# A list scheduler's table of durations replaced by the durations of the trace, in a two-layer diffusion step

## The chip, the cores and the metric

One core of a Trainium2 chip runs the whole program. The time is the device time of one execution in microseconds (us). Beside the timed runs there is one profiled execution, from which the rows of the trace are taken.

## The reference

The kernel computes one step of a small hybrid backbone with two layers on 384 tokens of width 1024: 256 latent tokens and 128 context tokens. Layer 0 projects once, then runs neighbourhood attention (8 heads) beside a bidirectional retention (8 heads). Layer 1 is a bidirectional gated linear recurrence (HGRN2, 8 heads of 128). Each is followed by a SwiGLU block, and every sub-layer is wrapped in two norms with modulation from a conditioning vector.

```python
hp = _rmsnorm(xp, norm_g[l, 0]) * (1.0 + sc1p) + sh1p
hs = _rmsnorm(xs, norm_g[l, 0]) * (1.0 + sc1s) + sh1s
...
xp = xp + gt1p * _rmsnorm(mp, norm_g[l, 1])
xs = xs + gt1s * _rmsnorm(ms, norm_g[l, 1])
hp = _rmsnorm(xp, norm_g[l, 2]) * (1.0 + sc2p) + sh2p
hs = _rmsnorm(xs, norm_g[l, 2]) * (1.0 + sc2s) + sh2s
xp = xp + gt2p * _rmsnorm(_swiglu(hp, w_ffn_in[l], w_ffn_out[l]), norm_g[l, 3])
xs = xs + gt2s * _rmsnorm(_swiglu(hs, w_ffn_in[l], w_ffn_out[l]), norm_g[l, 3])
```

## The kernel before

Activations stand transposed: 128 features on the partitions, 384 tokens along the free axis, eight such tiles k = 0 to 7. Weights come in 216 chunks of 128x1024 (eight 128x128 tiles each) by DMA into `wr`. Each chunk is split in two: ScalarE rounds it to `wh`, VectorE subtracts to get the rest `wl`. The input is split likewise into `hh` and `hl`. A product of float precision is then three matmuls, hh by wh, hh by wl and hl by wh. These are called **main products** here. There are 5088 of them, and the text counts them from 0: the first projection has 0 to 143, the two token-wise projections 144 to 287, the rest of layer 0's input projection up to 623, its output projection 624 to 815, the first SwiGLU 816 to 2399. Layer 1's input projection has 2400 to 3311, its output projection 3312 to 3503, and the second SwiGLU the rest.

Everything else on TensorE is side work: attention scores (`ka,qa`), transposes of the probabilities (`cb,as`), the retention (`qk`, `ro,vb`, `scr,cse`), the modulation (`mraw,sc` and, to turn the result, `ca,mev`), the sums of the norms (`scr,ca`, `acc,ca`, `rB,ca`), the spreading of a norm's factor over the partitions (`rs,cb`), and the eight mixers of layer 1. A mixer works through eight levels h = 0, 1, 2 up to 64. In each level TensorE multiplies the present pair of tiles (`XA` or `XB`, 64x64), VectorE picks from the product with a mask into `ac`, and ScalarE, GpSimd and VectorE make the next pair. After the last level come 128x128 products (`XB`, two transposes `cb,XB` and `cb,ZW`, `v,XA`, then nine into one bank beginning and ending with `at,v`) and a sum of squares (`scr,cb`). When four heads are through, `head_norm` takes a root, a reciprocal, splits the factors into `rh` and `rl`, and spreads them with `rh,bc` and `rl,bc`; then `o` is scaled, gated with `scr`, split into `hh` and `hl`, and only then can the output projection read it. The output projection begins with four of its eight outputs at once and walks over k, twelve main products to a k, so that its products 3312 to 3359 read heads 0 to 3, and those from 3360 on heads 4 to 7.

Nothing of this order is written by hand. Each piece of work is a generator (a stream) that yields operations. `Machine.run` (L174) looks at the next operation of each stream, computes when it could start from a clock for each engine and from the end of what it reads, and emits the one with the earliest start, in steps of 1/20 us, ties going by priority. `Machine.emit` (L127) then moves the engine's clock on by the operation's `cost`. So a cost decides nothing but the place of an instruction in the queue of its engine; on the chip each engine takes its queue in order and waits on semaphores. Added after an operation's end are fixed handover times (`LEAVE`, for VectorE 0.13 us), and 1.3 us for a change of ScalarE's function table.

A norm in mid program (class `Step`) has a path that nothing can hide: the last square is summed, a root and a reciprocal give the first factor, `rs,cb` spreads it, meanwhile three more sums feed a second root and reciprocal, a second `rs,cb` spreads that, and only then are `hh` and `hl` made for the next main product. While TensorE waits there, `keep_busy` sends fillers (`cb,ca`, results unused) and the modulation its products.

Of the kernel before, what the change touches and what calls it, by code (L numbers as in the profile page):

```python
# [30 lines left out]
F32R = mybir.dt.float32r  # L31
# [177 lines left out]
def width(ap):  # L209
    n = 1  # L210
    for s in ap.shape[1:]:
        n *= s
    return n


class Build:
# [4 lines left out]

    def mm(self, out, lhsT, rhs, start=True, stop=True):
        n = width(rhs)
        cost = n * (1 if rhs.dtype == F32R and n >= 256 else 4) / 2400
        cost *= {32: 0.3, 64: 0.56}.get(min(out.shape[0], lhsT.shape[0]), 1.0)
        return Op("PE", lambda: self.nc.tensor.matmul(out, lhsT=lhsT, rhs=rhs, start=start, stop=stop),  # L226
                  [out], [lhsT, rhs], cost + 0.004)

    def transpose(self, out, in_, ident):
        return Op("PE", lambda: self.nc.tensor.transpose(out, in_, ident), [out], [in_], 0.11)  # L230
# [1 line left out]
    def act(self, out, in_, func=AF.Copy, bias=None, scale=1.0, accum=None):  # L232
        kw = {"scale": scale}
        ins, outs = [in_], [out]
        if bias is not None:
            kw["bias"] = bias
            ins.append(bias)
        if not isinstance(scale, float):
            ins.append(scale)
        if accum is not None:  # L240
            kw["accum_out"] = accum
            outs.append(accum)
        table = None if func in (AF.Copy, AF.Identity, AF.Square) else func
        return Op("ACT", lambda: self.nc.scalar.activation(out, in_, func, **kw), outs, ins,  # L244
                  0.1 + width(in_) / 1200, table)

    def tt(self, out, a, b, op, pool=False):
        n = width(out)
        if pool:
            return Op("POOL", lambda: self.nc.gpsimd.tensor_tensor(out=out, in0=a, in1=b, op=op), [out], [a, b],  # L250
                      0.12 + n * 0.0021)
        return Op("DVE", lambda: self.nc.vector.tensor_tensor(out=out, in0=a, in1=b, op=op), [out], [a, b],  # L252
                  0.06 + n / 960)

    def ts(self, out, a, s1, op0, s2=None, op1=None):
        ins = [a] + [s for s in (s1, s2) if s is not None and not isinstance(s, float)]
        kw = {} if op1 is None else {"op1": op1}
        return Op("DVE", lambda: self.nc.vector.tensor_scalar(out=out, in0=a, scalar1=s1, scalar2=s2, op0=op0, **kw),  # L258
                  [out], ins, 0.19 + width(out) / 1920)

    def stt(self, out, a, s, b, op0, op1, accum=None):
        ins = [a, b] + ([] if isinstance(s, float) else [s])
        outs = [out] + ([] if accum is None else [accum])
        kw = {} if accum is None else {"accum_out": accum}
        return Op("DVE", lambda: self.nc.vector.scalar_tensor_tensor(out=out, in0=a, scalar=s, in1=b, op0=op0, op1=op1, **kw),  # L265
                  outs, ins, 0.1 + width(out) / 960)

    def copy(self, out, a):
        return Op("DVE", lambda: self.nc.vector.tensor_copy(out, a), [out], [a], 0.06 + width(out) / 960)

    def pcopy(self, out, a):
        return Op("POOL", lambda: self.nc.gpsimd.tensor_copy(out, a), [out], [a], 0.1 + width(out) * 0.0017)

    def recip(self, out, a):
        return Op("DVE", lambda: self.nc.vector.reciprocal(out, a), [out], [a], 0.1 + width(out) * 0.0065)

    def reduce_max(self, out, a):
        return Op("DVE", lambda: self.nc.vector.tensor_reduce(out=out, in_=a, axis=AX.X, op=ALU.max), [out], [a],
                  0.06 + width(a) / 960)

    def select(self, out, mask, data):
        return Op("DVE", lambda: self.nc.vector.copy_predicated(out, mask, data), [out], [mask, data, out],
                  0.06 + width(out) / 960)

    def zero(self, out):
        return Op("POOL", lambda: self.nc.gpsimd.memset(out, 0.0), [out], [], 0.1 + width(out) * 0.001)
# [91 lines left out]
def constants():  # L378
# [46 lines left out]
    for n, h in enumerate(LEVELS):  # L425
        m[:, n] = (s == tt) if h == 0 else ((s // (2 * h) == tt // (2 * h)) & (s // h != tt // h))
# [1298 lines left out]
```

## Time and profile before

| | us |
|---|---|
| timed runs | 1123.0, 1123.99, 1126.69 |
| median | 1123.99 |
| the profiled execution's own time | 1122.49 |
| its span, first to last instruction | 1120.3 |
| TensorE busy in the span | 1083.7 |
| VectorE busy | 811.7 |
| ScalarE busy | 551.7 |
| GpSimd busy | 131.8 |

Between span and time of the profiled execution lie 2.2 us that the trace doesn't show. In rows of the profile PE is TensorE, PEld its weight loads, DVE VectorE, ACT ScalarE, POOL GpSimd and SP the queue that issues DMAs. A row of the timeline has start, duration, engine, line, operation, what is written and read, the count of merged instructions, and in brackets idle time of the engine just before it with what ended it. Matmuls overlap in the pipeline, so that main products that each last 0.34 us follow each other at about half of that. A matmul in plain float appears as two passes.

### The profile page before, as it was taken

The page shows a single profiled execution, that of the slowest core. Times are in us where ns is not written, and L with a number is a line of the kernel's source. Part 1 is how long each engine was busy: PE and PEld are TensorE (multiplying, and loading weights), DVE is VectorE, ACT ScalarE, POOL GpSimd, SP SyncE. Part 2 cuts the span into 40 slices and gives each one's busy share as a digit, 9 for nine tenths or more (in the row PEclk, how much of TensorE's full clock was granted, in tenths as well). Part 3 has the DMA queues.
Part 4 walks back from the last instruction along what each step waited for, and adds up shares of the span by engine and source line. Part 5 has one row for each costly group of instructions (what it writes and reads, how often), then busy time and mean ns, then how long its engine had stood idle before and what let it go on. Part 6 is the DMA issues. An engine that isn't in the chain of part 4 may idle for free.

```text
span 1120.3 us, 18505 instructions
## 1 busy us (share of the span) xinstructions
PE 1083.7 (97%) x7172; PEld 1008.3 (90%) x7172; DVE 811.7 (72%) x1508; ACT 551.7 (49%) x1034; POOL 131.8 (12%) x143
## 2 busy tenths in 40 slices
PE   7999999999999999999999999999999999999996
PEld 5768877989999999999987988889989999999995
DVE  2599986688999998995887589996786444443434
ACT  4587654667333333323765456656575333333331
POOL 1220000000000000333024145341000000000001
PEclk9999999999999999999999999999999999999998
DMA  9966554254766666664432322212323333333331
GB/s 349 365 217 231 187 191 149 94 189 162 249 228 242 231 241 228 223 235 141 165 127 81 108 86 85 91 65 102 113 77 137 126 130 115 132 123 123 131 113 57
DMA packets 49687, 180.44 MB, mean 161 GB/s; under 512 B 6560, under 2 KB 13728, under 8 KB 43072
## 3 DMA queue, kind: packets, MB, share of 16 engines
q1 hardware_dynamic: 49536, 179.18, 45.5%
q8 instruction: 56, 0.92, 0.3%
q14 instruction: 31, 0.25, 0.1%
q0 software_dynamic: 64, 0.08, 0.0%
HBM read 174.79 MB, written 3.41 MB: 159 GB/s over the span
## 4 chain that ended last, share of the span: by engine, by line
PE 80%; DVE 12%; ACT 3%; issue 2%; DMA 2%; SPq 1%; POOL 0%; DVEq 0%; ACTq 0%; POOLq 0%
PE bank L226 79%; DVE wl L252 2%; DVE mscr L265 1%; DMA mraw<-in_w_mod 1%; ACT scr L244 1%; DVE XB L252 1%; PE bank L230 1%; DVE XA L252 1%; DVE scr L258 1%; DMA msb<-in_cB 1%; SPq L291 1%; DVE scr L252 0%; DVE T L258 0%; DVE XA L258 0%; DVE x L252 0%
## 5 line engine op out<-in xcount | busy, mean ns | idle before, releaser
L226 PE MATMUL bank<-hh,wh 128*128 128x384 f32 (+1 forms) x1248 | 429.2, 344 | 0.6 <-ACT hh L244 0.4
L226 PE MATMUL bank<-hh,wl 128*128 128x384 f32 (+1 forms) x1248 | 424.2, 340 | 0.0
L226 PE MATMUL bank<-hl,wh 128*128 128x384 f32 (+1 forms) x1248 | 391.8, 344 | 0.0
L252 DVE TENSOR_TENSOR wl<-wr,wh 128x1024 fp32r<-128x1024 f32 x216 | 273.2, 1266 | 127.8 <-ACT wh L244 127.6
L244 ACT ACTIVATE wh<-wr 128x1024 fp32r<-128x1024 f32 x216 | 228.1, 1057 | 150.9 <-PE bank L226 103.9
L226 PEld LDWEIGHTS bank<-hh,wh 128*128 128x128 f32 x1248 | 237.1, 190 | 7.8 <-ACT scr L244 2.4
L226 PEld LDWEIGHTS bank<-hl,wh 128*128 128x128 f32 x1248 | 232.0, 189 | 5.6 <-issue 1.7
L226 PEld LDWEIGHTS bank<-hh,wl 128*128 128x128 f32 x1248 | 236.7, 190 | 0.3
L265 DVE SCALAR_TENSOR_TENSOR mscr<-mraw,msb 128x1024 bf16<-128x1024 f32 x128 | 159.5, 1246 | 4.2 <-ACT msb L244 3.2
L226 PE MATMUL bank<-gh,wl 128*128 128x384 f32 x352 | 118.2, 336 | 1.9 <-DVE wl L252 1.9
L226 PE MATMUL bank<-gh,wh 128*128 128x384 f32 x352 | 117.6, 334 | 0.0
L226 PE MATMUL bank<-gl,wh 128*128 128x384 f32 x352 | 117.6, 334 | 0.0
L226 PEld LDWEIGHTS bank<-gh,wl 128*128 128x128 f32 x352 | 66.1, 188 | 3.5 <-DVE wl L252 3.5
L226 PEld LDWEIGHTS bank<-gh,wh 128*128 128x128 f32 x352 | 66.1, 188 | 0.0
L226 PEld LDWEIGHTS bank<-gl,wh 128*128 128x128 f32 x352 | 66.1, 188 | 0.0
L244 ACT ACTIVATE fs<-bank 128x384 f32<-128x384 f32 x44 | 21.1, 491 | 88.0 <-PE bank L226 88.0
L252 DVE TENSOR_TENSOR fs<-bank,fs 128x384 f32<-128x384 f32 x44 | 24.1, 557 | 38.0 <-PE bank L226 38.0
L244 ACT ACTIVATE gh<-fs 128x384 fp32r<-128x384 f32 x44 | 22.5, 520 | 58.0 <-DVE fs L252 58.0
L244 ACT ACTIVATE scr<-bank 128x384 f32<-128x384 f32 x44 | 21.9, 498 | 54.7 <-PE bank L226 54.7
L250 POOL TENSOR_TENSOR rB<-x,fy 128x384 f32<-128x384 f32 x1 | 1.8, 1782 | 381.4 <-DVE fy L258 381.4
L250 POOL TENSOR_TENSOR x<-x,fy 128x384 f32<-128x384 f32 x4 | 4.5, 1150 | 347.5 <-DVE fy L252 347.5
L250 POOL TENSOR_TENSOR ZW<-XB,TA 128x192 f32<-128x192 f32 x48 | 37.7, 806 | 37.8 <-ACT XA L244 17.8
(251 smaller groups left out, 1325.8 us busy)
## 6 DMA issues: line engine op xcount, KB each, us to landing
mraw<-in_w_mod SPq DMA_DIRECT2D x48, 1024.0 KB, 6.1
wr<-in_w_ffn_in SPq DMA_DIRECT2D x88, 512.0 KB, 3.3
wr<-in_w_ffn_out SPq DMA_DIRECT2D x44, 512.0 KB, 3.2
wr<-in_w_in_odd SPq DMA_DIRECT2D x40, 512.0 KB, 3.2
wr<-in_w_in_even SPq DMA_DIRECT2D x28, 512.0 KB, 4.4
wr<-in_w_out_even SPq DMA_DIRECT2D x8, 512.0 KB, 3.3
wr<-in_w_out_odd SPq DMA_DIRECT2D x8, 512.0 KB, 3.3
bias<-in_bias SPq DMA_DIRECT2D x8, 384.0 KB, 3.9
```

The source lines that it names most:

```text
L226: return Op("PE", lambda: self.nc.tensor.matmul(out, lhsT=lhsT, rhs=rhs, start=start, stop=stop), [out], [lhsT, rhs], cost + 0.004)
L230: return Op("PE", lambda: self.nc.tensor.transpose(out, in_, ident), [out], [in_], 0.11)
L244: return Op("ACT", lambda: self.nc.scalar.activation(out, in_, func, **kw), outs, ins, 0.1 + width(in_) / 1200, table)
L250: return Op("POOL", lambda: self.nc.gpsimd.tensor_tensor(out=out, in0=a, in1=b, op=op), [out], [a, b], 0.12 + n * 0.0021)
L252: return Op("DVE", lambda: self.nc.vector.tensor_tensor(out=out, in0=a, in1=b, op=op), [out], [a, b], 0.06 + n / 960)
L258: return Op("DVE", lambda: self.nc.vector.tensor_scalar(out=out, in0=a, scalar1=s1, scalar2=s2, op0=op0, **kw), [out], ins, 0.19 + width(o ...
L265: return Op("DVE", lambda: self.nc.vector.scalar_tensor_tensor(out=out, in0=a, scalar=s, in1=b, op0=op0, op1=op1, **kw), outs, ins, 0.1 + ...
L291: return Op("SP", lambda: self.nc.sync.dma_start(out, in_), [a for a in here if a is out], [a for a in here if a is in_], n / 355e3)
```

## The change

The functions that make operations give each its `cost`. The change replaces these figures for nearly all kinds and touches nothing else. A few of the lines:

```diff
-        cost = n * (1 if rhs.dtype == F32R and n >= 256 else 4) / 2400
+        cost = n / 2200 if rhs.dtype == F32R and n >= 256 else n / 600
...
-                  0.1 + width(in_) / 1200, table)
+                  0.17 + width(in_) / 1200, table)
...
-                  0.06 + n / 960)
+                  0.15 + n / 960)
```

A main product of 384 columns goes from 0.164 to 0.177 us, a VectorE operation of 384 columns from 0.46 to 0.55 (from 1.13 to 1.22 for a weight split), a ScalarE operation of 384 columns from 0.42 to 0.49, a GpSimd product of 192 columns from 0.52 to 0.76.

The main products keep their order. All else is placed anew around them. Counts on the engines stay, but for fillers (56 `cb,ca` before, 52 after, in fours) and ScalarE's table loads (18 before, 15 after). Three places follow.

TensorE at the last head of layer 1, before. The first factor `rh`, `rl` of heads 4 to 7 is spread here, in the middle of the main products of the last input projection (`hh,wh` and the like):

```order
L226 MATMUL bank_69<-hl,wh_110 128x384
L226 MATMUL bank_70<-rh,bc_4560 128x384
L226 MATMUL bank_70<-rl,bc_4560 128x384
L226 MATMUL bank_69<-hh,wh_110 128x384
L226 MATMUL bank_69<-hh,wl_113 128x384
L226 MATMUL bank_69<-hl,wh_110 128x384
L226 MATMUL bank_64<-hh,wh_111 128x384
L226 MATMUL bank_64<-hh,wl_114 128x384
L226 MATMUL bank_65<-hh,wh_111 128x384
L226 MATMUL bank_65<-hh,wl_114 128x384
L226 MATMUL bank_67<-rh,bc_4560 128x384
L226 MATMUL bank_67<-rl,bc_4560 128x384
```

The same after, from the last main product ahead of k = 4 of the output projection (3359) to the first behind it (some rows of the nine products, and of the four spreads, are not shown):

```order
L226 MATMUL bank_65<-hl,wh_112 128x384
L226 MATMUL bank_69<-XB_4584 64x64 x6
L226 MATMUL bank_68<-XA_4583 64x64 x6
L226 MATMUL bank_63<-XB_4584 128x128 x2
L230 MATMUL bank_63<-cb,XB_4584 128x128
L230 MATMUL bank_63<-cb,ZW_4585 128x128
L226 MATMUL bank_63<-v,XA_4583 128x128 x2
L226 MATMUL bank_64<-at_4587,v 128x128
...
L226 MATMUL bank_64<-scr_91,cb 32x96 x4
L226 MATMUL bank_69<-rh,bc_4562 128x384
L226 MATMUL bank_69<-rl,bc_4562 128x384
...
L226 MATMUL bank_67<-hh,wh_110 128x384
```

The four spreads stood at main products 3309, 3316, 3326 and 3335 and now all stand at 3360. So do the last two levels of head 7 (`XB`, `XA`) and its products; those of 128x128 began at 3258 before. No main product stands between them.

VectorE in layer 0, where the retention's norm feeds the output projection, before (`rs` is the norm's factor, `qk` the retention's output, `va` its gate, `wl` a weight split):

```order
L275 RECIPROCAL rs_88<-rs_88 128x96
L252 TENSOR_TENSOR hl<-qa,hh 128x384
L252 TENSOR_TENSOR scr_91<-rs_88,cb 128x384
L252 TENSOR_TENSOR wl_115<-wr_109,wh_112 128x1024
L252 TENSOR_TENSOR hl<-qa,hh 128x384
L252 TENSOR_TENSOR qk<-qk,bank_66 128x384
L252 TENSOR_TENSOR qk<-qk,va 128x384
```

And after (`mscr` is a modulation product by VectorE, of 1024 columns):

```order
L275 RECIPROCAL rs_88<-rs_88 128x96
L265 SCALAR_TENSOR_TENSOR mscr_132,macc_134<-mraw_105,msb_131 128x1024
L252 TENSOR_TENSOR wl_114<-wr_108,wh_111 128x1024
L252 TENSOR_TENSOR scr_92<-rs_88,cb 128x384
L265 SCALAR_TENSOR_TENSOR mscr_132,macc_134<-mraw_105,msb_131 128x1024
L252 TENSOR_TENSOR qk<-qk,bank_70 128x384
L265 SCALAR_TENSOR_TENSOR mscr_132,macc_134<-mraw_105,msb_131 128x1024
L252 TENSOR_TENSOR qk<-qk,va 128x384
```

Three modulation products have come into this path. On TensorE the spread that feeds `qk<-qk,bank` has gone from main product 635 to 672, and 672 is the first that reads its result.

TensorE at the norm ahead of the second SwiGLU (main product 3504), before:

```order
L226 MATMUL bank_65<-scr_95,ca 32x96 x4
L226 MATMUL bank_68<-rB,ca 32x96 x4
L226 MATMUL bank_64<-mraw_105,sc 32x256 x4
L226 MATMUL bank_68<-scr_93,ca 32x96 x4
L226 MATMUL bank_68<-acc_86,ca 32x96 x4
L226 MATMUL bank_68<-scr_92,ca 32x96 x4
L226 MATMUL bank_66<-rs_88,cb 128x96 x4
L226 MATMUL bank_64<-mraw_104,sc 32x256 x8
L226 MATMUL bank_67<-rs_89,cb 128x96 x4
```

And after:

```order
L226 MATMUL bank_70<-scr_92,ca 32x96 x4
L226 MATMUL bank_67<-mraw_105,sc 32x256 x4
L226 MATMUL bank_65<-rs_88,cb 128x96 x4
L226 MATMUL bank_66<-rB,ca 32x96 x4
L226 MATMUL bank_66<-scr_91,ca 32x96 x4
L226 MATMUL bank_66<-acc_86,ca 32x96 x4
L226 MATMUL bank_66<-scr_95,ca 32x96 x4
L226 MATMUL bank_67<-mraw_104,sc 32x256 x8
L226 MATMUL bank_67<-ca,mev 128x2 x4
L226 MATMUL bank_69<-rs_89,cb 128x96 x4
```

The four sums that feed the second factor have gone behind the spread of the first (`rs_88,cb`). At the norm of main product 816 the same has happened, with `ca,mev` also ahead of them; at 2400 these rows have kept their order.

More of the change, by code (lines that the diff above doesn't have):

```diff
@@ L223, in mm @@
         n = width(rhs)
-        cost = n * (1 if rhs.dtype == F32R and n >= 256 else 4) / 2400
+        cost = n / 2200 if rhs.dtype == F32R and n >= 256 else n / 600
         cost *= {32: 0.3, 64: 0.56}.get(min(out.shape[0], lhsT.shape[0]), 1.0)
         return Op("PE", lambda: self.nc.tensor.matmul(out, lhsT=lhsT, rhs=rhs, start=start, stop=stop),
-                  [out], [lhsT, rhs], cost + 0.004)
+                  [out], [lhsT, rhs], cost + 0.002)
     def transpose(self, out, in_, ident):
@@ L250, in tt @@
             return Op("POOL", lambda: self.nc.gpsimd.tensor_tensor(out=out, in0=a, in1=b, op=op), [out], [a, b],
-                      0.12 + n * 0.0021)
+                      0.3 + n * 0.0024)
         return Op("DVE", lambda: self.nc.vector.tensor_tensor(out=out, in0=a, in1=b, op=op), [out], [a, b],
-                  0.06 + n / 960)
+                  0.15 + n / 960)
     def ts(self, out, a, s1, op0, s2=None, op1=None):
@@ L258, in ts @@
         return Op("DVE", lambda: self.nc.vector.tensor_scalar(out=out, in0=a, scalar1=s1, scalar2=s2, op0=op0, **kw),
-                  [out], ins, 0.19 + width(out) / 1920)
+                  [out], ins, 0.21 + width(out) / 1920)
     def stt(self, out, a, s, b, op0, op1, accum=None):
@@ L265, in stt @@
         return Op("DVE", lambda: self.nc.vector.scalar_tensor_tensor(out=out, in0=a, scalar=s, in1=b, op0=op0, op1=op1, **kw),
-                  outs, ins, 0.1 + width(out) / 960)
+                  outs, ins, 0.15 + width(out) / 960 + (0.0 if accum is None else 0.08))
     def copy(self, out, a):
-        return Op("DVE", lambda: self.nc.vector.tensor_copy(out, a), [out], [a], 0.06 + width(out) / 960)
+        return Op("DVE", lambda: self.nc.vector.tensor_copy(out, a), [out], [a], 0.15 + width(out) / 960)
     def pcopy(self, out, a):
@@ L274, in recip @@
     def recip(self, out, a):
-        return Op("DVE", lambda: self.nc.vector.reciprocal(out, a), [out], [a], 0.1 + width(out) * 0.0065)
+        return Op("DVE", lambda: self.nc.vector.reciprocal(out, a), [out], [a], 0.13 + width(out) * 0.0065)
     def reduce_max(self, out, a):
         return Op("DVE", lambda: self.nc.vector.tensor_reduce(out=out, in_=a, axis=AX.X, op=ALU.max), [out], [a],
-                  0.06 + width(a) / 960)
+                  0.15 + width(a) / 960)
     def select(self, out, mask, data):
         return Op("DVE", lambda: self.nc.vector.copy_predicated(out, mask, data), [out], [mask, data, out],
-                  0.06 + width(out) / 960)
+                  0.15 + width(out) / 960)
     def zero(self, out):
```

## The prediction

> **What bounds the kernel now.** First the head of the page, which gives each engine's busy time in the span.
>
> ```profile
> span 1120.3 us, 18505 instructions
> PE 1083.7 (97%) x7172; PEld 1008.3 (90%) x7172; DVE 811.7 (72%) x1508; ACT 551.7 (49%) x1034; POOL 131.8 (12%) x143
> ```
>
> TensorE is busy for 1083.7 of 1120.3 us, and its operations stay the same but for four fillers. So the change can only move what TensorE loses: some 37 us without work, half-clock stretches, and the extra time of going from main products to side work and back. Where an engine beside it is full is told by the windows (from:to, length, busy of PE, PEld, DVE, ACT, POOL with instruction counts, granted clock, DMA share, GB/s).
>
> ```profile
> 480.00:500.00 20.00, 18.83 (x104) 17.87 (x105) 19.83 (x29) 6.40 (x9) 6.37 (x4) 1.00 0.67 239
> 700.00:720.00 20.00, 19.72 (x170) 18.22 (x171) 19.97 (x46) 12.96 (x30) 7.00 (x10) 1.00 0.22 72
> ```
>
> VectorE is full in the first SwiGLU (480 to 500) and in the mixers (700 to 720); only there can its order hold TensorE. What TensorE waits for is told by the waits (total us, times, longest).
>
> ```profile
> PE bank L226 <- DMA mraw<-in_w_mod: 9.3, 2, 6.9
> PE bank L226 <- DVE wl L252: 2.0, 6, 0.6
> PE bank L226 <- DVE XB L252: 1.6, 4, 0.7
> PE bank L230 <- ACT qk L244: 0.6, 1, 0.6
> ```
>
> The first is the start (6.9) and one wait of 2.4 in mid program. All four together are 13.5 us, 6.9 of them at the start where nothing can be done: little to gain. A scheduler that places side work so that nothing waits is near its floor; one that places it wrongly has no floor. So I count what becomes late.
>
> **Is the new table nearer the truth?** These two rows follow each other on VectorE.
>
> ```profile
> 753.77 1.21 DVE L252 TENSOR_TENSOR wl<-wr,wh 128x1024 fp32r<-128x1024 f32 x1
> 754.91 0.55 DVE L252 TENSOR_TENSOR scr<-bank,scr 128x384 f32<-128x384 f32 x1
> ```
>
> The split lasts 1.21, but the next starts 1.14 after its start: the old cost (1.13) is the engine's step, the new one (1.22) the duration. So the model's VectorE gets slower than the chip's by about 0.08 an operation, and side work is put later than it could be, by 30 to 50 main products in the attention and 10 to 140 in the mixers.
>
> **The start.**
>
> ```profile
> 11.31 1.94 PE L226 MATMUL bank<-mraw,sc 128*32 128x256 f32 x16
> 13.18 0.69 PE L226 MATMUL bank<-hh,wh 128*128 128x386 f32 x1
> 14.03 0.37 ACT L244 ACTIVATE mev<-bank 128x256 f32<-128x256 f32 x1
> ```
>
> The first main product begins at 13.18. In the new order the second `ca,mev` stands ahead of it, and reads the `mev` that ScalarE ends at 14.40. The main product then begins some 1.3 later (0 if ScalarE comes to it sooner, 1.6 at most with the product's own time): **+1.3**.
>
> **The wait for the modulation.**
>
> ```profile
> 162.92 0.44 PE L226 MATMUL bank<-hl,wh 128*128 128x384 f32 x1
> 165.72 1.02 PE L226 MATMUL bank<-mraw,sc 128*32 128x256 f32 x8 [2.36 <-DMA mraw<-in_w_mod]
> 166.00:168.00 2.00, 2.00 (x20) 0.70 (x12) 0.51 (x2) 0.00 (x0) 0.00 (x0) 0.50 0.95 375
> 168.00:170.00 2.00, 2.00 (x20) 0.95 (x12) 2.00 (x4) 0.00 (x0) 0.00 (x0) 0.69 0.35 47
> ```
>
> At main product 528 TensorE waits 2.36 us for a load that SP has issued behind weights. The product now stands at 672, 144 main products of 0.18 us or 26 us later; on SP its load goes back behind only some weights and `ro<-qk`. The wait goes: **-2.4**. After it the granted clock is 0.50 for 2 us and 0.69 for 2: (1-0.50)x2+(1-0.69)x2 = 1.6, **-1.6**. Next there are the main products of 528 themselves, whose weights ended no wait in this row. The attention's wait for `qk` goes too, as its transposes move back: **-0.6**.
>
> By the Trainium skill, "TensorE: Matmul & The Clock Gate", What's actually happening, the clock falls after an idle window of about 3.4 us. The wait here was 2.36 and the clock fell all the same, so the trace speaks against that length as a threshold. By the page only the wait is saved, and the sum would be 1.6 higher.
>
> **Switches.** Going into side work and back has a price.
>
> ```profile
> 765.61 0.34 PE L226 MATMUL bank<-hh,wl 128*128 128x384 f32 x1
> 765.79 0.34 PE L226 MATMUL bank<-hl,wh 128*128 128x384 f32 x1
> 766.06 0.57 PE L226 MATMUL bank<-XA 128*64 128x64 f32 x12
> 766.56 0.44 PE L226 MATMUL bank<-hh,wh 128*128 128x384 f32 x1
> ```
>
> Main products start 0.18 apart; the `XA` products start 0.27 after one, and the main product behind them lasts 0.44 where the others last 0.34: 0.09 + 0.10, about 0.2 for a switch. The new order has 70 runs of side work in the mixers where there were 83: 13 x 0.2, **-2.6**. In the attention 32 for 42, half of them transposes that I price at nothing: 10 x 0.1, **-1.0**. The waits for `XB` go, as their readers stand later: **-1.6**.
>
> **The first output projection.** The path from spread to `hh` now has a `mscr` in it.
>
> ```profile
> 79.16 1.22 DVE L265 SCALAR_TENSOR_TENSOR mscr<-mraw,msb 128x1024 bf16<-128x1024 f32 x1
> 201.67 0.56 DVE L252 TENSOR_TENSOR qk<-qk,bank 128x384 f32<-128x384 f32 x1 [0.92 <-PE bank L226]
> 202.86 0.56 DVE L252 TENSOR_TENSOR qk<-qk,va 128x384 f32<-128x384 f32 x1 [0.63 <-ACT va L244]
> 203.68 0.51 ACT L244 ACTIVATE hh<-qk 128x384 fp32r<-128x384 f32 x1
> ```
>
> The spread moves from main product 635 to 672, and 672 itself reads the result. TensorE, with all main products queued behind, waits 0.56 + 1.22 + 0.56 + 0.51 = 2.85: **+2.8** (0 if the spread's k = 4 wasn't the first needed, 4 with handovers and a second `mscr`).
>
> **The three norms.**
>
> ```profile
> 238.44 1.05 PE L226 MATMUL bank<-ca,mev 128*128 128x2 f32 x8
> 239.53 0.17 DVE L252 TENSOR_TENSOR mod<-bank,bmod 128x8 f32<-128x8 f32 x1 [1.11 <-PE bank L226]
> 820.65 0.35 PE L226 MATMUL bank<-rB,ca 128*32 128x96 f32 x8
> 822.81 1.13 PE L226 MATMUL bank<-rs,cb 128*128 128x96 f32 x8 [0.28 <-DVE rs L275]
> ```
>
> At 3504 the four sums for the second factor now wait behind `rs,cb` of the first: two groups of two sums by the row of 0.35 (0.17 each, 0.7), and about 1.0 of the 1.13 of `rs,cb` itself, whose end overlaps: **+1.7**. At 816 `ca,mev` (1.05) comes on top, but the 1.11 that VectorE waited for it is no longer in the path: **+1.8**. At 2400 the order is kept: 0. Below 0 these can't go, for the second factor needs all four sums; the fillers hide nothing, since they stand behind.
>
> **The first SwiGLU.** Its six waits for `wl` came where by the order a `mscr` of 1.22, priced at 1.17, stood ahead of a split: **-2.0** from the row above. But three more splits go ahead of the last `mscr` (from split 94 to 97 of 102), with VectorE at 19.83 of 20.
>
> **The last head.** This term decides. In the new order nothing of a main product stands between head 7's sixth level and the spreads, all at 3360, and 3360 reads what they give. TensorE takes its queue in order, so this chain can't begin before 3359 has been issued. Its pieces, from the rows of the same operations before:
>
> ```profile
> 764.98 0.36 DVE L282 COPY_PREDICATED ac<-msk,bank 128x192 f32<-128x192 uint8 x1
> 770.07 0.48 DVE L258 TENSOR_SCALAR XA<-XB,TA 128x128 f32<-128x128 f32 x2
> 770.90 0.61 PE L226 MATMUL bank<-XB 128*128 128x128 f32 x4
> 774.88 0.39 PE L226 MATMUL bank<-at,v 128*128 128x128 f32 x2
> 777.98 1.28 ACT L244 ACT_TABLE_LOAD   x1
> 778.21 0.37 PE L226 MATMUL bank<-scr,cb 128*32 128x96 f32 x8
> 779.28 0.38 ACT L244 ACTIVATE ss<-ss,eps 128x96 f32<-128x96 f32 x1
> 779.69 0.75 DVE L275 RECIPROCAL ss<-ss 128x96 f32<-128x96 f32 x1 [0.71 <-ACT ss L244]
> 782.43 0.55 DVE L252 TENSOR_TENSOR rl<-rr,rh 128x384 fp32r<-128x384 f32 x1
> 783.89 0.34 PE L226 MATMUL bank<-rh,bc 128*128 128x384 f32 x1
> 784.44 0.61 DVE L265 SCALAR_TENSOR_TENSOR o<-o,gnm,bank 128x384 f32<-128x384 f32 x1
> ```
>
> - The mask's select (764.98) to the last level's end (770.55) took 5.6 with other work in it; the operations alone give some 1.6. I take 3.3, with one `wl` ahead of them.
> - `XB` to `at,v`: 770.90 to 774.88 is 4.0, with 12 main products of 0.18 (2.2) in it. Where these hid part of ScalarE's copies they don't come off in full: between 1.8 and 4.0 I take 2.3.
> - `at,v` to `scr,cb`: 774.88 to 778.21 is 3.3, with 7 main products (1.3) in it: between 2.0 and 3.3 I take 2.6, the middle.
> - `scr,cb` to the reciprocal, past the table load: 1.5. Reciprocal's start to the end of `rl` (782.98): 3.3 with a gate ahead, 2.3 without.
> - `rh,bc` 0.4; then `o` (0.61), the gate (384 columns, 0.56 as `qk<-qk,va`) and `hh` (0.51, as at 203.68), with three handovers of 0.2: 2.3.
>
> That is 3.3 + 2.3 + 2.6 + 1.5 + 2.3 + 0.4 + 2.3 = 14.7. In it lies TensorE's own work, which was paid before as well: two levels 1.0, the 128x128 products 3.1, sums and spreads 1.6: 5.7. So **+9.0** (7 with the first three pieces at the low ends but for a `wl`, 13.6 with the rows' own spacing). After so long a wait the clock falls as it did at 166: **+1.6**.
>
> The row of 777.98 and that of 779.28 are back to back: the load ends at 779.26. The Trainium skill, "ScalarE: Activation LUTs", What ACT_TABLE_LOAD costs, puts a drain of 1.38 us beside the 1.28 of the load. No drain stands behind the load here; by the page the chain, and the sum, would be 1.4 longer.
>
> **The sum.** 1.3 - 2.4 - 1.6 - 0.6 - 1.0 + 2.8 + 1.8 + 1.7 - 2.0 - 1.6 - 2.6 + 9.0 + 1.6 = **+6.4**. On the profiled execution's 1122.5 (span 1120.3 and 2.2 around it) that is 1128.9; the median of the runs, 1124.0, lies 1.5 above that execution, so the forecast is **1130.4**. A measurement of this kernel tells about 0.3%, 3.4 us, from no change: the bounds are 1120.6 and 1127.4.
>
> **Rivals.**
>
> 1. *Switches are dear: faster.* I price 23 switches and the `XB` waits at 5.2 in all. A switch that also waits for `XB` costs 0.2 + 1.6/4 = 0.6. If every saved one were worth 0.50, the gains would cancel the sum; from 0.65 on the change is faster by over 0.3%. At 0.7 the sum is 6.4 - (16.1 - 5.2) = -4.5: **1119.5**. For it: VectorE is full at 700 to 720, so that side work there is often not ready. Against: TensorE is busy for 19.72 of the same 20 us. Chance 0.13.
> 2. *The late chains are shorter than the rows: no change.* ScalarE and VectorE have little to do around 3360, the chain costs 7 and the clock holds (-3.6), and the spread at 672 is covered by what stands between (-2.8): sum 0.0, **1124.0**. For it: the rows were taken with other work between. Against: no operation of the chain can be left out. Chance 0.20.
> 3. *VectorE overflows in the first SwiGLU: slower still.* The three splits pushed behind `mscr` meet an engine at 19.83 of 20; TensorE waits some 2 a split, +6, and the clock falls at 672 and 816 too, +3.2: **1139.6**. Against: the waits there were only 2.0. Chance 0.12.
>
> The change not doing what it says is part of all: the table holds durations where the engine's step is shorter, as shown above.
>
> **How the numbers follow.** The forecast has 0.55; its own range is 1126.5 to 1136, the tail from 7 to 13.6. It is inside 0.3% with 0.03. Faster: 0.13. Same: 0.20 + 0.03 = 0.23. Slower: 0.52 + 0.12 = 0.64. The range reaches to rivals 1 and 3: 1119 to 1141.
>
> **What would show it.** In the timeline after, a wait of 7 to 11 us in pieces between main products 3359 and 3360, near 795, with the clock at half behind it; no wait for `mraw` near 165; the first main product near 14.5; a wait for ScalarE's `hh` near 210; the stretches without main products ahead of 816 and 3504 each longer by nearly 2; fewer waits for `wl` and `XB`. If the wait at 3360 is under 4 us, or the mixers gain over 10, the prediction is wrong.

## The result and the profile after

| | before | after |
|---|---|---|
| median of the timed runs, us | 1125.21 | 1142.47 |
| range, 4 runs each | 1123.0 to 1126.69 | 1138.96 to 1144.14 |
| ratio | | 1.0151, 95% interval 1.0134 to 1.0167 |

The first three runs of before are those of the table above, and a fourth (1126.43) has been added. The change makes the kernel 17.3 us slower. The sign was forecast; the size was not: +6.4 stood in the sum, and 1142.5 lies above the range, which ended at 1141.

The head of the page of the changed kernel, and the mean granted clock over its span (0.993 before):

```profile
span 1142.4 us, 18492 instructions
PE 1091.7 (96%) x7164; PEld 1016.9 (89%) x7164; DVE 807.1 (71%) x1508; ACT 546.6 (48%) x1031; POOL 138.1 (12%) x143
core 0: 1142.4 us, clock 0.985
```

TensorE does less work (7164 instructions for 7172) and is busy 8 us longer: its operations got slower, not more. The other 14 us are idle. Its waits after (in us, times, longest), some of them:

```profile
PE bank L226 <- DVE rs L275: 7.5, 6, 2.0
PE bank L226 <- DMA mraw<-in_w_mod: 7.4, 2, 7.2
PE bank L226 <- DVE wl L252: 3.4, 3, 1.6
PE bank L226 <- ACT rh L244: 3.2, 1, 3.2
PE bank L226 <- ACT mev L244: 3.1, 3, 1.2
PE bank L226 <- ACT hh L244: 2.6, 2, 2.2
PE bank L226 <- DVE XB L252: 2.5, 2, 2.1
```

Three of these before:

```profile
PE bank L226 <- DVE rs L275: 3.3, 5, 1.2
PE bank L226 <- ACT mev L244: 1.3, 1, 1.3
PE bank L226 <- ACT hh L244: 0.4, 1, 0.4
```

The load in mid program is gone, as forecast (`mraw` 7.4 is the start alone). In its place stand new or longer waits: `rh` and most of `XB`, which are the last head, `mev` at the start (two, where there was one) and at 3504, `hh` at 672, and `rs`, most of it at the norms. The waits for `wl`, forecast to go, are fewer but longer: 3.4 us instead of 2.0.

The last head, in the timeline after (a selection of rows). Start and duration are the first two numbers; the main products up to 3359 have just been issued:

```profile
793.84 0.57 PE L226 MATMUL bank<-XB 128*64 128x64 f32 x12
794.45 0.37 DVE L282 COPY_PREDICATED ac<-msk,bank 128x192 f32<-128x192 uint8 x1 [0.66 <-PE bank L226]
796.81 1.19 PE L226 MATMUL bank<-XB 128*128 128x128 f32 x4 [2.05 <-DVE XB L252]
799.69 1.22 PE L226 MATMUL bank<-v,XA 128*128 128x128 f32 x4 [0.47 <-ACT XA L244]
800.70 0.63 PE L226 MATMUL bank<-at,v 128*128 128x128 f32 x2
801.12 0.64 PE L226 MATMUL bank<-XA,v 128*128 128x128 f32 x2
...
803.81 0.39 PE L226 MATMUL bank<-at,v 128*128 128x128 f32 x2
805.12 1.28 ACT L244 ACT_TABLE_LOAD   x1
805.16 0.37 PE L226 MATMUL bank<-scr,cb 128*32 128x96 f32 x8 [0.96 <-ACT o L244]
...
806.42 0.37 ACT L244 ACTIVATE ss<-ss,eps 128x96 f32<-128x96 f32 x1
806.82 0.75 DVE L275 RECIPROCAL ss<-ss 128x96 f32<-128x96 f32 x1 [0.90 <-ACT ss L244]
...
808.76 0.56 DVE L252 TENSOR_TENSOR rl<-rr,rh 128x384 fp32r<-128x384 f32 x1 [0.59 <-ACT rh L244]
808.78 0.69 PE L226 MATMUL bank<-rh,bc 128*128 128x384 f32 x1 [3.25 <-ACT rh L244]
...
812.43 0.69 PE L226 MATMUL bank<-hh,wh 128*128 128x384 f32 x1 [0.45 <-ACT hh L244]
```

From the level's product (793.84) to main product 3360 (812.43) pass 18.6 us; the prediction had 14.7. The windows of the same stretch (length, busy of PE, PEld, DVE, ACT, POOL, granted clock, DMA share, GB/s) show what the clock did there:

```profile
796.00:803.00 7.00, 5.20 (x21) 4.53 (x22) 2.02 (x10) 2.04 (x7) 0.00 (x0) 0.55 0.26 94
803.00:807.00 4.00, 1.57 (x17) 1.16 (x15) 0.43 (x2) 2.53 (x4) 0.00 (x0) 0.93 0.00 0
807.00:814.00 7.00, 4.77 (x14) 3.96 (x15) 5.57 (x11) 1.52 (x3) 0.00 (x0) 0.52 0.00 0
```

The clock does not fall behind the chain but inside it, twice, so that TensorE's own links get slower: `at,v` and `XA,v` start 0.42 apart. Before, with the clock full, it was 0.22, as these rows and that of 774.88 in the prediction show:

```profile
773.55 0.61 PE L226 MATMUL bank<-v,XA 128*128 128x128 f32 x4
775.10 0.39 PE L226 MATMUL bank<-XA,v 128*128 128x128 f32 x2
776.67 0.39 PE L226 MATMUL bank<-at,v 128*128 128x128 f32 x2
```

### The profile page after: what moved, and what is told of

Read it like the earlier page. It is cut to its first block, busy times and chain, and to the rows that moved or that the text cites. A ratio compares the mean times of both kernels' runs of the same rounds, so it can differ in the third digit from the quotient of the medians.

```text
span 1142.4 us, 18492 instructions
## 1 busy us (share of the span) xinstructions
PE 1091.7 (96%) x7164; PEld 1016.9 (89%) x7164; DVE 807.1 (71%) x1508; ACT 546.6 (48%) x1031; POOL 138.1 (12%) x143
## 4 chain that ended last, share of the span: by engine, by line
PE 80%; DVE 11%; ACT 3%; issue 3%; DMA 1%; SPq 1%; POOL 0%; DVEq 0%; ACTq 0%; POOLq 0%
PE bank L226 80%; DVE wl L252 2%; DVE mscr L265 2%; SPq L291 1%; ACT scr L244 1%; DMA wr<-in_w_in_even 1%; DVE scr L252 1%; PE bank L230 1%; ACT hh L244 1%; DVE XB L252 1%; DVE fy L252 1%; DVE rs L275 0%; DMA ro<-qk 0%; ACT L244 0%; ACT wh L244 0%
## 5 line engine op out<-in xcount | busy, mean ns | idle before, releaser
L226 PE MATMUL bank<-hh,wh 128*128 128x384 f32 (+1 forms) x1248 | 431.0, 345 | 2.6 <-ACT hh L244 2.6
L226 PE MATMUL bank<-hh,wl 128*128 128x384 f32 (+1 forms) x1248 | 425.7, 341 | 0.0
L226 PE MATMUL bank<-hl,wh 128*128 128x384 f32 (+1 forms) x1248 | 390.5, 343 | 0.9 <-DVE hl L252 0.9
L252 DVE TENSOR_TENSOR wl<-wr,wh 128x1024 fp32r<-128x1024 f32 x216 | 269.8, 1249 | 116.1 <-ACT wh L244 115.9
L226 PEld LDWEIGHTS bank<-hh,wh 128*128 128x128 f32 x1248 | 238.1, 191 | 10.0 <-ACT hh L244 3.7
L226 PEld LDWEIGHTS bank<-hl,wh 128*128 128x128 f32 x1248 | 233.3, 190 | 6.0 <-issue 2.0
L226 PEld LDWEIGHTS bank<-hh,wl 128*128 128x128 f32 x1248 | 237.9, 191 | 0.3
L265 DVE SCALAR_TENSOR_TENSOR mscr<-mraw,msb 128x1024 bf16<-128x1024 f32 x128 | 162.1, 1266 | 4.9 <-DMA wr<-in_w_ffn_in 2.7
L226 PE MATMUL bank<-gh,wl 128*128 128x384 f32 x352 | 117.9, 335 | 3.4 <-DVE wl L252 3.4
L226 PE MATMUL bank<-gh,wh 128*128 128x384 f32 x352 | 117.6, 334 | 0.0
L226 PE MATMUL bank<-gl,wh 128*128 128x384 f32 x352 | 117.6, 334 | 0.0
L226 PEld LDWEIGHTS bank<-gh,wl 128*128 128x128 f32 x352 | 66.1, 188 | 4.3 <-DVE wl L252 4.3
L226 PEld LDWEIGHTS bank<-gh,wh 128*128 128x128 f32 x352 | 66.1, 188 | 0.0
L226 PEld LDWEIGHTS bank<-gl,wh 128*128 128x128 f32 x352 | 66.1, 188 | 0.0
```

## The experiments

Most kernels below carry both costs of an operation, the new one (`cost`) and the old one (`was`), and a rule picks one. `count` is the number of operations that TensorE has been given so far. The order thus equals that of the change, or that of before, up to the point where the rule switches. The line numbers in their rows are higher by 7 (L233 is L226).

```diff
+def COST(op, count):
+    return op.cost if count < 1188 else op.was
...
-            cost = op.cost
+            cost = COST(op, self.count)
+            self.count += op.eng == "PE"
```

My theory (A): the time is lost at a few places where a chain is stacked right ahead of its first reader, and at the half clock there. Rivals: it is lost a little everywhere (B), or only by a backlog that one stage hands to the next (C).

### Which stage

The three rules were `count < 1188`, `1192 <= count < 2852` and `count >= 2852`.

> The new costs are used until main product 816 has been reached (layer 0 up to and with the norm ahead of the first SwiGLU), the old ones from there on; the order up to 816 is that of the change. Theory A (few places): the time is lost where a chain is stacked against its first reader, and at the half clock behind it. The two traces stand +5.8 us apart at main product 815 and +8.7 at 816, so this kernel should be 7 to 10 us slower than before (ratio about 1.0075), with the stalls at 672 and 816 as in the change. Theory B (spread): every piece of side work is a little late everywhere, in proportion to the side work; layer 0 has about a third of it, so some 5 to 6 us. Theory C (carry over): a stage is only slow because the one before left a backlog; then the parts add up to clearly less than the whole of 17.

Measured: 1129.74 against 1124.59, +5.2 us, ratio 1.0049 (1.0032 to 1.0065). That is below the 7 to 10 of theory A and within the 5 to 6 of B, so by itself it does not favour A. Its trace has the places that A named: against the first profile of before, main products 671 to 690 lose 4.7 us and 815 to 816 lose 2.1, while 180 to 671 gain 5.0.

> The new costs only from main product 816 to 2400 (the first SwiGLU), the old ones before and after; the order up to 816 is that of before. Theory A: nothing is stacked here; the traces differ by +0.2 us over this stretch, so within 2 us of before (0.998 to 1.002), waits for wl by VectorE at one or two places of 1 to 2 us. Theory B: some 3 us slower, as VectorE is full here. My prediction had -2.0 for this stretch.

Measured: 1124.25, -0.3 us, 0.9998 (0.9987 to 1.0008). Neither the -2.0 of the prediction nor the 3 of theory B.

> The new costs only from main product 2400 on (layer 1 and the second SwiGLU). The order then puts 70 products between main products 3359 and 3360 (39 in the change). Theory A: the tail of head 7 decides; the traces differ by +13 us from 2400 to the end, so 12 to 18 us slower, nearly all of it between 3312 and 3384 and at 3504. Theory B: 8 us, over the whole mixer stage. Theory C: much less than 13.

Measured: 1140.08, +15.5 us, 1.0132 (1.0115 to 1.015), as A had it.

The parts add up to 20.4, the whole is 17.3: no hint that a stage is slow only through the one before it, so C falls. B falls too, since the first SwiGLU, where VectorE is full, costs nothing. Layer 1 carries three quarters. (The third part stacks 70 products where the change stacks 39, so it is not the change's own tail; but the change's 17.3 less the 4.4 of the kernel below that has VectorE's old costs in layer 1 also leaves 12.9, three quarters.)

### Duration or step

```diff
+    return op.cost - 0.07 if op.eng in ("DVE", "ACT") else op.cost
```

> The new costs, but 0.07 us less for every operation of VectorE and ScalarE: the step at which operations follow each other back to back, not the duration of one. By the order nothing stands at 3360, and the spreads feeding the output projection of layer 0 go ahead of 672 again (630, 648, 666). If the change is slow because durations are taken for steps, this kernel is within 4 us of before (0.997 to 1.004). If new figures as such disturb an order fitted to the old ones, it is 5 us slower or more.

Measured: 1138.05, +13.5 us, 1.0121 (1.0106 to 1.0136). My expectation fell. The 0.07 decides whether the tail is stacked at 3360: main products 3312 to 3384 take as long here as before. But the kernel loses elsewhere, as the timeline's waits of TensorE show:

```profile
139.12 1.22 PE L233 MATMUL bank<-qd,s 128*128 128x256 f32 x2 [2.17 <-DVE qd L259]
168.19 1.24 PE L233 MATMUL bank<-qk 64*128 64x128 f32 x3 [3.88 <-DVE ro L259]
275.31 1.05 PE L233 MATMUL bank<-ca,mev 128*128 128x2 f32 x8 [0.72 <-ACT mev L251]
278.37 0.44 PE L233 MATMUL bank<-hh,wh 128*128 128x384 f32 x1 [2.01 <-ACT hh L251]
```

The first two are the retention, whose products stand ahead of what VectorE has ready; the last two are the modulation, put at main product 924, where the next `hh` needs its result. A table nearer to the engine's step is not a better order.

### Which engine

```diff
+    return op.was if count >= 2848 and op.eng == "DVE" else op.cost
```

> The new costs throughout, but VectorE's old ones from main product 2400 on. By the order nothing stands at 3360 any more (the spreads of heads 4 to 7 are at 3314 to 3348). Theory A (the stacked tail is the loss of layer 1, and VectorE's clock in the model stacks it): 10 to 13 us faster than the change, so 5 to 7 us slower than before (ratio 1.0045 to 1.0065), like the kernel with the new costs up to 816 only. Rival (layer 1's loss comes from all engines' costs alike): about half of it stays, 10 us slower than before.

Measured: 1129.25 against 1124.85, +4.4 us, 1.0048 (1.0031 to 1.0065). As theory A had it: with VectorE's old costs in layer 1 alone, what is left is layer 0's loss.

```diff
+    return op.cost if op.eng != "DVE" else op.was
```

> VectorE's costs as before everywhere, those of TensorE, ScalarE and GpSimd new. By the order the spread for k = 4 goes ahead of 672 again (630 to 650), nothing stands at 3360, the start is as before, and the modulation goes to 552 and 816. Theory A' (VectorE's costs alone do the harm): within 3 us of before (0.997 to 1.003). Rival, after the run with 0.07 us less for each operation (13 us slower with nothing at 3360): the old order is a fitted one and any other table loses at places of its own; then 5 us slower or more, with waits of TensorE for the retention's qk between 430 and 530 or for ca,mev behind a norm.

Measured: 1125.33, +0.5 us, 0.9998 (0.9982 to 1.0014). With VectorE's costs left alone, those of the other three engines do no harm to the time as a whole. But that is a balance of losses and gains, and the waits that the rival named are there:

```profile
136.52 1.13 PE L233 MATMUL bank<-qd,s 128*128 128x256 f32 x4 [2.27 <-DVE qd L259]
180.00 1.45 PE L233 MATMUL bank<-qk 64*128 64x128 f32 x4 [2.15 <-DVE ro L259]
```

The profile, of the slowest of the ten runs, is 12.0 us behind the first of before at main product 560 and 5.7 at 864, then gains 3.1 up to 3384. From 3384 to 3520 it loses 3.3, as much as the change: what is lost at the norm of 3504 does not need VectorE's costs.

```diff
+    return op.cost if count >= 2852 and op.eng == "DVE" else op.was
```

> Only VectorE's costs are new, and only from main product 2400 on; all else is old. The order puts 94 products between main products 3359 and 3360 (39 in the change): head 7 with nearly all its levels. Theory A' (VectorE's costs alone stack the tail, and each level that is stacked costs its latency): the change's trace has one level at 3.0 us from its product to the next one's start, of which 0.5 is TensorE's own. With some five levels more than in the change, at 1.5 to 2.5 each, 18 to 25 us slower than before, more than the 15.5 of the third experiment. Rival (the costs of the other engines have a share): less than 13.

Measured: 1143.41 against 1124.60, +18.8 us, 1.0164 (1.0144 to 1.0185). VectorE's costs alone, in layer 1 alone, cost as much as the whole change. Three profiles now have the tail stacked to different heights. Worked out from the starts of main products in their traces, against the first profile of before:

```
products between 3359 and 3360    39 (change)   70 (from 2400)   94 (this one)
gained from 2416 to 3336, us          9.5          14.5             15.9
lost from 3336 to 3384, us           21.1          29.7             35.7
net loss, us                         11.6          15.2             19.8
```

Much of what the mixers seem to gain is work put off, and about twice as much comes back at 3360, where no main product lies beside it (1.8 to 2.0 times if the second profile of before is taken, 2.0 to 2.2 here).

```diff
-            end = c[op.eng] = t + cost
+            c[op.eng], end = t + cost, t + cost + op.cost - op.was
```

Here `cost` is the old one: the engine is free after the old duration, the reader may start after the new one.

> An operation occupies its engine in the model for the old cost, and its result is ready after the new one. By the order only the four spreads of the last head stand at 3360, not the levels and products ahead of them. Theory A: what stacks the tail is the engine's clock; the chain at 3360 is short here (from the spread to hh 3.65 us in the change's trace, less TensorE's own 1.4), so 2 to 6 us slower than before. Rival (readiness counts as much as the clock): 10 us or more.

Measured: 1134.43 against 1124.85, +9.6 us, 1.0077 (1.0062 to 1.0093). Between the two. The stacked rest is short, as expected:

```profile
799.69 0.44 PE L233 MATMUL bank<-rh,bc 128*128 128x384 f32 x1 [1.56 <-ACT rh L251]
802.98 0.69 PE L233 MATMUL bank<-hh,wh 128*128 128x384 f32 x1 [1.00 <-ACT hh L251]
```

But from 3336 to 3384 this trace still loses 10.4 us: 2.7 in the waits shown and one of 0.16, the rest side work that has moved there and the half clock. So the engine's clock stacks the levels, and the later readiness alone is enough to stack the spreads. The tail is not most of the 9.6, though: less the 6.2 gained from 2416 to 3336 it costs 4.3. In the same trace 3.8 are lost up to 864, 3.1 from there to 2400 and 3.0 from 3384 to 3520.

### Single terms of the sum

The rule `count < 120`:

> The new costs for the first 120 operations of TensorE only (to main product 70), the old ones after; from main product 118 on the order is that of before. It isolates the term of the start. My prediction had +1.3. The traces of the change and of the first experiment stand +4.9 and +4.6 us apart from before at main product 144: a second ca,mev with its wait, and the half clock of the start lasting 6 us longer. So 1.3 (ratio 1.0012) by the prediction, 4.6 (1.0041) by the traces.

Measured: 1124.47 against 1124.85, ratio 0.9997 (0.9987 to 1.0008). In its trace main product 144 starts 3.1 us later than before, so the start is later than the 1.3 of the prediction; but the time as a whole shows nothing: the interval leaves at most 0.9 us, less than either number expected. This trace had no fall of the clock at main product 528, and the first of before had one. Whether a later start always avoids such a fall can't be told from one profile; this stays open.

```diff
-            yield lambda: mods.pe and not W.hungry
+            yield lambda: mods.pe and not W.hungry and not 20 <= W.used < 28
```

> The costs of before; the modulation's products are held back between weight chunks 20 and 28, so that TensorE no longer waits for their load at main product 528. By the order they go to 816 and 924. It isolates the term of -2.4 and -1.6. By the prediction 4 us are gained at 528; in the trace of the fourth experiment the modulation at 924 had waits of 0.7 and 2.0 us and a half clock behind them. So: at 528 4 us less in the trace, lost again at 924; as a whole within 3 us of before. If the modulation costs nothing at 924, 3 to 4 us faster (0.9965).

Measured: 1129.53 against 1124.60, +4.9 us, 1.0048 (1.0031 to 1.0065), outside the 3 us expected.

```profile
164.58 0.49 PE L226 MATMUL bank<-qk 64*128 64x128 f32 x2 [1.61 <-DVE ro L252]
266.91 1.05 PE L226 MATMUL bank<-ca,mev 128*128 128x2 f32 x8 [0.72 <-ACT mev L244]
269.97 0.44 PE L226 MATMUL bank<-hh,wh 128*128 128x384 f32 x1 [2.01 <-ACT hh L244]
```

With the wait for the load (2.36) out of the way, TensorE waits 1.61 at the same place for VectorE's `ro`, and the clock falls all the same. I had looked for what is late next among the main products; it was the retention's side work. And at 924 the modulation loses what the table less 0.07 had shown, 2.7 us of waits. No order that was tried is faster than before.

### The same kernels again

> The changed kernel once more, for a second profile. The falls of the clock so far lie on a grid of 3.413 us whose phase differs by execution, behind windows with TensorE busy for under about half. If that holds, the falls at 3360 come again, those at 672, 816 and 3504 may come or not, and main products without side work keep their times.

> The kernel before once more, for a second profile. The first profiled execution (1122.5) was at the low end of its runs (median 1124.8 of 22). If falls of the clock make the difference, this one has them at the waits of main products 147, 174 or 528, and stands some 2 us above the first where the order is the same.

Measured: 1141.54 and 1125.17 us. The second profile of before stands 2.7 us above the first at the last main product, with 1.4 of it between main products 144 and 180 and 1.2 between 500 and 560. That is near the 2 expected, and at 174 and 528 as expected, though not at 147. The windows show the clock there:

```profile
165.00:172.00 7.00, 5.41 (x33) 2.48 (x34) 4.98 (x11) 1.79 (x4) 0.00 (x0) 0.57 0.76 269
63.00:67.00 4.00, 3.52 (x8) 2.80 (x9) 4.00 (x8) 3.81 (x8) 2.12 (x2) 0.57 0.95 370
```

In the other direction, the fall that the first profile had at 538, behind the norm of main product 2400, is missing here (-1.6). From 576 to 2400 the two traces agree to 0.2 us. Another +1.6 between 2544 and 2688, in the mixers, goes with no fall; two waits, of 0.57 for `XB` and 0.46 for `XA`, stand there, and why they came was not followed up. The second profile of the change is 2.6 us below its first, by the start and by a fall at main product 672 that it lacks; the falls in the tail are there again, and so are those at 816 and 3504.

## Why the prediction was wrong

The two second profiles differ by 16.4 us in time, near the 17.3 of the medians, so they are the pair to compare. The starts of main products in them, change less before, beside the terms of the sum:

```
main products    prediction               predicted   measured
0 to 144         start                       +1.3       +3.6
144 to 815       load, clock, qk, switches,
                 spread at 672               -2.8       -2.8
815 to 864       first norm                  +1.8       +2.6
864 to 2400      wl in the first SwiGLU      -2.0       +0.6
2400 to 3384     mixers, tail, clock         +6.4       +9.4
3384 to 3520     norm at 3504                +1.7       +3.3
sum                                          +6.4      +16.7
```

Most steps had the right places: what was named as getting later got later. The sizes were too small in five of the six rows. The term that was furthest out, as far as this can be told, is **the clock.** The sum let it come out even, -1.6 at 528 and +1.6 in the tail. The mean granted clock of the pair, before and after:

```profile
core 0: 1123.0 us, clock 0.992
```

```profile
core 0: 1139.8 us, clock 0.986
```

The share that the clock took is (1 - 0.992) x 1123.0 = 9.0 us before and (1 - 0.986) x 1139.8 = 16.0 us after, some 7 us more (6.6 with the clocks of the traces not rounded). Where TensorE waits in such a stretch nothing is lost by it, so this is the most that the clock can be of the 10.3 that the sum lacks. TensorE's busy time grows by 4.3 us in this pair (1085.1 to 1089.4), with eight instructions fewer; the other 12.4 of the 16.7 are idle. At least 3.7 of the 10.3 are thus something else, 2.6 of them in the first SwiGLU. Point by point:

- **The last head** (mis-sized). Two pieces came out much longer. From `XB` to `at,v` 2.3 was taken and 3.9 measured; from `at,v` to `scr,cb` 2.6 was taken and 4.5 measured, with a wait of 0.96 for ScalarE. In both, TensorE's own links ran at half clock. `XB` and `v,XA` lasted 1.19 and 1.22, where the rows before have 0.61 each: 1.2 more. The nine products from `at,v` on took 3.5 (800.70 to 804.20) instead of 2.2 (774.88 to 777.06): 1.3 more. An estimate from these rows for full clock is therefore 2.7 and 3.1, near the pieces as taken. So what failed is mainly the clock, put down as 1.6 behind the chain; inside it, it cost some 2.5 in these two pieces alone. (The timeline has 14 main products from 770.90 to 774.88 and not the 12 that the prediction took off.) The other pieces held: level 3.0 for 3.3, past the root 1.7 for 1.5, reciprocal to `rl` 2.5 for 2.3, from there to the main product 3.1 for 2.7. Together 18.6 less the 5.7 that was TensorE's own is 12.9, where 9.0 + 1.6 stood. The mixers' own gain is then, by difference, 12.9 - 9.4 = 3.5, near the 4.2 forecast. VectorE is busy for only 2.0 of 7 us here (796 to 803): its order can hold TensorE where it is not full, against the prediction's opening.

- **The norm at 3504** (mis-sized). The step itself is +1.4 in the trace, near 1.7. Behind it the first profile of the change shows the clock at half for 7 us, which the sum didn't have, +1.8. The second has it too. Of six profiles with the old costs at this norm, the one with the new costs up to 816 has a fall of the clock here as well; so a fall at this place does not need the new costs.

```profile
841.60 1.13 PE L226 MATMUL bank<-rs,cb 128*128 128x96 f32 x8 [1.57 <-DVE rs L275]
848.00:855.00 7.00, 6.39 (x40) 5.95 (x41) 5.97 (x11) 5.38 (x11) 0.00 (x0) 0.52 0.22 76
```

- **The start** (mis-sized). The wait for `mev` is there as forecast:

```profile
14.23 0.36 ACT L244 ACTIVATE mev<-bank 128x256 f32<-128x256 f32 x1
14.65 1.01 PE L226 MATMUL bank<-ca,mev 128*128 128x2 f32 x4 [1.16 <-ACT mev L244]
15.52 0.67 PE L226 MATMUL bank<-hh,wh 128*128 128x386 f32 x1
```

  The first main product begins 2.3 later, not 1.3, since `ca,mev` itself (0.9) is in the path as well. And the clock becomes full at 21.8 us (19.2 in the second profile) instead of 15.7. By the experiment on the start alone at most 0.9 us of this remain in the time as a whole; what makes up for the rest stays open.

- **The first SwiGLU** (failed). The waits for `wl` didn't go; the experiment from 816 to 2400 had no gain either. The step "these six waits came from a cost set too low" was an argument from the order. Five of the six, 1.8 us, stood in the first SwiGLU, the longest (0.58) at main product 2185. With the new costs there are three, 3.4 us, the longest (1.65) at 2185 again and one of 1.38 at 2305; and the kernel with new costs up to 816 only has one of 2.20 at 2185, with the old cost at work there. What sets them stays open.

- **Layer 0 from 144 to 815** (the sum right, in part by luck). With the two first profiles the same stretch is +0.9 and not -2.8, as the falls of the clock in it differ. Its parts are out as well: 144 to 671 gains 8.1 in the pair where 5.6 was forecast, and 671 to 690 loses 4.7 where 2.8 was, for TensorE's own work came to 672 as well. The chain itself came as worked out: from `qk<-qk,bank` to the main product 2.8.

```profile
210.02 0.55 DVE L252 TENSOR_TENSOR qk<-qk,bank 128x384 f32<-128x384 f32 x1 [0.30 <-PE bank L226]
210.49 1.22 DVE L265 SCALAR_TENSOR_TENSOR mscr<-mraw,msb 128x1024 bf16<-128x1024 f32 x1
211.63 0.55 DVE L252 TENSOR_TENSOR qk<-qk,va 128x384 f32<-128x384 f32 x1
212.22 0.52 ACT L244 ACTIVATE hh<-qk 128x384 fp32r<-128x384 f32 x1 [2.99 <-DVE qk L252]
212.80 0.57 PE L226 MATMUL bank<-hh,wh 128*128 128x384 f32 x1 [2.17 <-ACT hh L244]
```

  But the term of -2.4 and -1.6 for the load can't be had by itself: in the experiment that held the modulation, another wait and another fall took its place.

- **Is the new table nearer the truth?** That the tail is stacked because durations were taken for steps fits the table less 0.07, which unstacks it. That this explains the whole loss is refuted by the same run.

- **The rivals.** By the 3.5 above, switches were not dearer; the chains were not shorter, and VectorE didn't overflow in the first SwiGLU. The time came nearest to the third rival (1139.6), mostly by other means: of the two falls of the clock that it named, the one at 816 came in both profiles of the change (at 250.5 and 247.9), the one at 672 in the first alone.

## What to carry to other kernels

In a list scheduler a cost moves an instruction; it does not make the model true. Here VectorE's old figures and the places that they gave hung together: each of the two tables that changed them throughout lost 13 us or more, at places of its own, and the one that left them alone lost nothing as a whole. So judge such a table by the order that it gives, above all by what stands between a long chain and its first reader. Where a chain is stacked on an engine that takes its queue in order, charge the slower clock to the links inside it, and not only to what comes behind.

## What the runs showed of the hardware

The granted clock falls on a grid. In the 14 traces every fall begins a whole number of 3.413 us after the moment at which the clock first became full: in the first profile of before the clock is full at 15.7 and falls at 165.8 and 537.9, which are 44 and 153 such steps later. Up to the last main product there are 50 falls, each of one, two or three steps. I took TensorE's busy share (by its matmuls, whose ends are modelled) in each step up to there that ended at full clock. Of 28 with a share under 0.46 the clock fell behind 27; of 28 between 0.46 and 0.60 behind 10; of 4377 above it behind 13, all of these next to a norm, where TensorE runs fillers and small sums. The share alone does not decide: the step that ends at 63.4 in the first profile of before and the one that ends at 63.5 in the second both have 0.44, and the clock fell behind the second alone. The moment of the first full clock differs by execution (14.4 to 16.3 us with the order of before), so a wait of 2 us may lie in one step or across two. That would fit the norm at 2400, followed by a fall in one profile of before and not in the other: a step ends 0.05 us after the start of main product 2400 in the first and 1.85 us ahead of it in the second. It does not explain 174, where the two lie alike, and at 528 the clock fell in both, for one step and for two. The phase itself was not set by any experiment.

The Trainium skill, "TensorE: Matmul & The Clock Gate", What's actually happening, gives an idle window of about 3.4 us. The prediction read this as the length of a wait and found the trace against it. The grid's 3.413 us agrees with it as the length of the window; a window need not be idle throughout, here under about 0.46 busy was enough in 27 of 28.
